# High-part products first, 2048 wide splits and VectorE over both token tiles in the FFN of a diffusion layer

## The chip, the cores and the metric

The kernel runs on one core of one Trainium2 chip. TensorE multiplies, VectorE and ScalarE work element by element, SyncE (SP) issues the transfers, and all five engines run side by side, held together by semaphores. The metric is the device time of one execution in microseconds; the time of a kernel is the median of its runs.

## The reference

One layer of a diffusion backbone on 256 latent tokens of width 2048, in fp32: attention with modulated input, then the SwiGLU feed-forward net (FFN), each with a gated residual and a layer norm. The change touches the FFN:

```python
x = layer_norm(DN_ALPHA * x + g1 * (heads @ w_out[layer]), ln1_g[layer], ln1_b[layer])
u = modulate(x, sh2, sc2)                                   # 256 x 2048
x = layer_norm(DN_ALPHA * x + g2 * ((jax.nn.silu(u @ w_gate) * (u @ w_up)) @ w_down), ln2_g[layer], ln2_b[layer])
```

w_gate and w_up are 2048 x 5632, w_down is 5632 x 2048. sh2, sc2 and g2 are rows of `silu(c) @ w_ada + b_ada`.

## The kernel before, in words

An fp32 product is made of three float32r products: each operand is the sum of a high part (its cast to float32r) and a low part (the rest), and `mm3` adds hi x high, lo x high and hi x low into one accumulator. The activations are the stationary operand of TensorE (`lhsT`, 128 x 128), the weights the moving one (128 x 512). The activations' parts are `u2h` and `u2l` for gate and up, `hTh` and `hTl` for the down projection; `fh` and `fl` hold sums of them (below).

The weights come in tiles of 4 x 128 rows by 512 columns, 1 MB, which SyncE loads into `raw` (four buffers). `split_raw` makes the two parts of a tile in two pieces of 1024: for each, ScalarE casts it into a `hi` tile (L331) and VectorE subtracts that into a `lo` tile (L332). The pool `whl` has four slots each for `hi` and `lo`, 1024 wide. A cast into a slot waits for the last matmul that read the slot's previous content; a load into `raw` waits for the subtraction that read it last. A tile makes 24 matmuls: 4 row blocks x 2 token tiles (`NT`, the 256 tokens are two tiles of 128) x 3.

Until about 400 us a planner (`Flow`) sets the order of attention. Behind it the FFN is written out in the order of the program, and the tile framework's scheduler places the instructions on each engine and puts in the semaphores. Its stages are:

- `first_half`: the first row blocks of gate and up (`project`), beside the steps that make the modulation. The sums go to `spill` tiles.
- Five pairs of 512 wide gate and up columns (`f0` = 0, 2, 4, 6, 8). In each a `folded` generator does four row blocks by four of the gate in 7 instead of 8 products (a Strassen-like scheme); its pieces are 1024 wide, 6 matmuls each, and VectorE makes sums of the weights in `raw` in between. The tiles of `up` run in between (`between`), then the other gate tiles. `shared` adds one of the seven products to the second gate's spill, once per token tile. `residual_base` loads ln1's scale and bias into the single buffer `lgb` (two loads, each spread over all partitions) and makes the base of the residual of 512 columns, with two operations per token tile (L1491, L1492). It is called four times, ahead of the pairs 4, 6 and 8, and the scheduler has drawn all four forward into the first pair.
- `flip_steps`: the gated product of gate and up, a transpose through a scratch buffer in HBM (`put`, `get`), and `place`, which splits the transposed tile into `hTh` and `hTl`, once per token tile.
- The down projection in four groups of 512 output columns (`down_steps`, `last_steps`), with two more `folded` pairs (`down_pair`). `gate2_steps` makes the rows of g2 beside it in four steps of 512: VectorE sums rows of `w_ada` into `adav`, and `split_rows` splits and sums them with a matrix of ones (L478, L479).
- In `last_steps` the last three tiles (`g0` to `g0 + 2`) are multiplied by g2 as weights, and accumulate into banks that ScalarE has filled with the residual (`seed`, L1901). `ending` is the last layer norm.

## Time and profile before

| | |
|---|---|
| device time, median of 3 runs | 1123.49 us (1122.72 to 1123.51) |
| span of the profiled execution | 1121.0 us |
| TensorE busy | 1102.3 us (98%) |
| VectorE busy | 903.4 us (81%) |
| ScalarE busy | 598.7 us (53%) |
| TensorE's share of the chain that ended last | 91% |
| mean share of the 16 DMA engines for the loads' queue | 81.7% |

The span reaches from the first instruction to the last; the device time is that of the whole execution, with what lies around it, so the two are 2.5 us apart. A busy TensorE is not one at its peak, since matmuls overlap; how many start in a stretch says more. Idle time of an engine costs only where another waits for it.

### The profile page before, as it was taken

What the parts mean: (1) busy time and instruction counts of PE and PEld (TensorE: products, weight loads), DVE (VectorE), ACT (ScalarE), POOL (GpSimd) and SP (SyncE); (2) the same over time, 40 slices, a digit from 0 to 9 for tenths busy, and PEclk for the clock granted to TensorE, in tenths of its full rate; (3) what the DMA queues carried; (4) which work ended last, traced back from release to release, by engine and by line L of the source; (5) the groups of instructions that cost most, each with busy time, mean ns of one, the idle gap of its engine ahead of it and who ended that gap; (6) DMA issues with size and microseconds to landing.
All of it is one profiled execution on the core that took longest, in us unless ns stands there. A gap on an engine that the chain in (4) does not pass through costs nothing.

```text
span 1121.0 us, 14130 instructions
## 1 busy us (share of the span) xinstructions
PE 1102.3 (98%) x5213; PEld 883.7 (79%) x5213; DVE 903.4 (81%) x1133; ACT 598.7 (53%) x875; POOL 36.7 (3%) x82
## 2 busy tenths in 40 slices
PE   8999999999999999999999999999999999999995
PEld 6766688777887788888888878888888888888884
DVE  5763589899999888787778697988996987689876
ACT  3341554878685356444475565767766344444442
POOL 1000030110100001000000000000000000000000
PEclk9999999999999999999999999999999999999998
DMA  9999999778999778999956677777776998669742
GB/s 321 394 385 375 393 362 377 247 234 274 345 332 395 249 269 321 348 318 296 336 182 216 223 220 266 234 246 271 228 267 216 329 348 293 228 235 379 287 149 76
DMA packets 178317, 321.26 MB, mean 287 GB/s; under 512 B 8732, under 2 KB 43196, under 8 KB 175943
## 3 DMA queue, kind: packets, MB, share of 16 engines
q1 hardware_dynamic: 177528, 320.03, 81.7%
q8 instruction: 41, 0.67, 0.2%
q10 hardware_dynamic: 720, 0.33, 0.1%
q14 instruction: 28, 0.23, 0.1%
HBM read 304.07 MB, written 16.25 MB: 286 GB/s over the span
## 4 chain that ended last, share of the span: by engine, by line
PE 91%; DMA 3%; DVE 2%; ACT 1%; SPq 1%; issue 0%; ACTq 0%; DVEq 0%
PE acc L341 20%; PE acc L343 20%; PE acc L342 20%; PE wk L342 8%; PE wk L341 8%; PE wk L343 8%; PE wk L1081 2%; PE wk L654 2%; DMA raw<-in_w_in_dram 2%; DVE lo L332 1%; DMA lgb<-in_ln_g_dram 1%; PE wk L755 1%; SPq L569 1%; DMA xt<-in_x_dram 0%; PE wk L1414 0%
## 5 line engine op out<-in xcount | busy, mean ns | idle before, releaser
L331 ACT CAST hi<-raw 128x1024 fp32r<-128x1024 f32 x279 | 290.7, 1054 | 256.4 <-PE acc L343 162.4
L332 DVE TENSOR_TENSOR lo<-raw,hi 128x1024 fp32r<-128x1024 f32 x279 | 336.1, 1220 | 103.6 <-ACT hi L331 101.4
L341 PE MATMUL acc<-hi,u2h 128*128 128x512 f32 x390 | 152.5, 391 | 0.0
L343 PE MATMUL acc<-hi,u2l 128*128 128x512 f32 x390 | 151.7, 390 | 0.7 <-DVE u2l L1669 0.7
L342 PE MATMUL acc<-lo,u2h 128*128 128x512 f32 x390 | 151.8, 389 | 0.0
L603 ACT CAST hi<-raw 128x1024 fp32r<-128x1024 f32 (+1 forms) x86 | 87.4, 1030 | 113.8 <-DMA raw<-in_w_in_dram 63.2
L466 DVE SCALAR_TENSOR_TENSOR adav<-raw,cs,adav 128x512 f32<-128x512 f32 (+1 forms) x128 | 121.4, 949 | 8.4 <-DMA raw<-in_w_ada_dram 4.9
L606 DVE TENSOR_TENSOR lo<-raw,hi 128x1024 fp32r<-128x1024 f32 (+1 forms) x86 | 101.3, 1194 | 16.3 <-ACT hi L603 15.5
L341 PE MATMUL acc<-hi,uh 128*128 128x512 f32 x256 | 103.7, 405 | 1.3 <-ACT uh L769 0.8
L342 PE MATMUL wk<-lo,u2h 128*128 128x512 f32 x264 | 103.1, 390 | 0.5 <-DVE lo L332 0.5
L343 PE MATMUL wk<-hi,u2l 128*128 128x512 f32 x264 | 102.7, 389 | 0.0
L341 PE MATMUL wk<-hi,u2h 128*128 128x512 f32 x264 | 102.2, 389 | 0.0
L342 PE MATMUL acc<-lo,uh 128*128 128x512 f32 x256 | 100.5, 392 | 0.6 <-DVE lo L606 0.6
L343 PE MATMUL acc<-hi,ul 128*128 128x512 f32 x256 | 100.1, 391 | 0.4 <-DVE ul L784 0.4
L341 PE MATMUL acc<-hi,hTh 128*128 128x512 f32 x236 | 92.0, 390 | 0.4 <-ACT acc L1901 0.4
L342 PE MATMUL acc<-lo,hTh 128*128 128x512 f32 x236 | 91.8, 389 | 0.0
L343 PE MATMUL acc<-hi,hTl 128*128 128x512 f32 x236 | 91.8, 389 | 0.0
L343 PEld LDWEIGHTS acc<-hi,u2l 128*128 128x128 f32 x390 | 73.2, 188 | 16.2 <-DVE u2l L1669 1.1
L341 PEld LDWEIGHTS acc<-hi,u2h 128*128 128x128 f32 x390 | 73.2, 188 | 16.1 <-ACT u2h L1668 0.8
L342 PEld LDWEIGHTS acc<-lo,u2h 128*128 128x128 f32 x390 | 73.2, 188 | 15.1
L341 PEld LDWEIGHTS acc<-hi,uh 128*128 128x128 f32 x256 | 48.1, 188 | 19.0 <-issue 5.6
L342 PEld LDWEIGHTS wk<-lo,u2h 128*128 128x128 f32 x264 | 49.5, 188 | 12.0 <-DVE lo L332 1.8
(277 smaller groups left out, 1748.0 us busy)
## 6 DMA issues: line engine op xcount, KB each, us to landing
raw<-in_w_ada_dram SPq DMA_DIRECT2D x70, 1024.0 KB, 7.7
raw<-in_w_gate_dram SPq DMA_DIRECT2D x44, 1024.0 KB, 6.7
raw<-in_w_up_dram SPq DMA_DIRECT2D x44, 1024.0 KB, 5.6
raw<-in_w_down_dram SPq DMA_DIRECT2D x44, 1024.0 KB, 5.8
raw<-in_w_ada_dram SPq DMA_DIRECT2D x48, 512.0 KB, 5.9
raw<-in_w_in_dram SPq DMA_DIRECT2D x18, 1024.0 KB, 11.0
raw<-in_w_out_dram SPq DMA_DIRECT2D x16, 1024.0 KB, 6.5
pd<-hx SPq DMA_DIRECT2D x64, 128.0 KB, 3.4
```

The costliest lines, as they stand in the source:

```text
L331: nc.scalar.copy(hi[:, :n], raw[:, s : s + n])
L332: nc.vector.tensor_tensor(lo[:, :n], raw[:, s : s + n], hi[:, :n].bitcast(F32), op=ALU.subtract)
L341: nc.tensor.matmul(ps, lhsT=xh, rhs=w[0], start=first, stop=False, skip_group_check=seeded)
L342: nc.tensor.matmul(ps, lhsT=xh, rhs=w[1], start=False, stop=False, skip_group_check=seeded)
L343: nc.tensor.matmul(ps, lhsT=xl, rhs=w[0], start=False, stop=last, skip_group_check=seeded)
L466: nc.vector.scalar_tensor_tensor(a[:, c : c + piece], raw[:, f : f + piece], cs[:, 4 * (g * (G4 * NB // w) + j) + 2, None], a[:, c : c + p ...
L569: nc.sync.dma_start(room.t, w[k0 * P : (k0 + 1) * P, c0 : c0 + width])
L603: nc.scalar.copy(hl.hi[:, :n], raw.t[:, s : s + n])
L606: nc.vector.tensor_tensor(hl.lo[:, :n], raw.t[:, s : s + n], hl.hi[:, :n].bitcast(F32), op=ALU.subtract)
L654: nc.tensor.matmul(bank.t[32 * j : 32 * j + 32, :width], lhsT=cs[:, 4 * k + 2 - 2 * i : 4 * k + 34 - 2 * i], rhs=raw.t[:, c * width : (c + ...
L755: nc.tensor.transpose(ps.t[:, (j * 2 + t) * P : (j * 2 + t + 1) * P], src, ident)
L1081: nc.tensor.matmul(o_ps.t[:, : 2 * P].rearrange("p (g q) -> p g q", q=32), lhsT=v, rhs=pv[:, k], start=k == 0, stop=k == 3)
```

## The change

It has three parts. `products` takes the place of `mm3` in the FFN: for a tile it issues all matmuls with the high part of the weights, with both parts of the activations, then those with the low part. `split_raw` casts and subtracts a whole tile of 2048 in one instruction each, into a pair of neighbouring slots of one tile per part, `parts`, with four slots of 1024; `part_pair` hands them out in turn, and a 2048 wide piece starts at an even slot. (Pieces of 1024, as in `folded`, and the rows of 512 take one slot each; the planner gives its casts planned slots.) And `residual_base`, `shared`, the gated product and `place` treat both token tiles in one instruction; `gate2_steps` has two steps of 1024 instead of four of 512.

```diff
-    whl = ctx.enter_context(tc.tile_pool(name="whl", bufs=HL_BUFS))
+    whl = ctx.enter_context(tc.tile_pool(name="whl", bufs=1))
...
+    parts = {c: whl.tile([P, HL_BUFS, SUB * NB], F32R, tag=c, name=c) for c in ("hi", "lo")}
+    turns = [0]
+
+    def part_pair(n):
+        wide = SUB * NB
+        if n > wide:
+            turns[0] += turns[0] % 2
+        i = turns[0] % HL_BUFS
+        turns[0] += -(-n // wide)
+        return [parts[c].rearrange("p b n -> p (b n)")[:, i * wide : i * wide + n] for c in ("hi", "lo")]
...
     def split_raw(raw, spare=False):
-        for s in range(0, raw.shape[-1], SUB * NB):
+        for s in range(0, n, SUB * NB if spare else n):
...
-                hi = whl.tile([P, SUB * NB], F32R, tag="hi", name="hi")
-                lo = whl.tile([P, SUB * NB], F32R, tag="lo", name="lo")
-            nc.scalar.copy(hi[:, :n], raw[:, s : s + n])
-            nc.vector.tensor_tensor(lo[:, :n], raw[:, s : s + n], hi[:, :n].bitcast(F32), op=ALU.subtract)
+                hi, lo = part_pair(n)
+            split(hi, lo, raw[:, s : s + m])
...
+    def products(banks, w, first, last, seeded=False):
+        for j, x in enumerate(banks):
+            for i, (ps, xs) in enumerate(x):
+                for h in xs:
+                    nc.tensor.matmul(ps, lhsT=h, rhs=w[j][0], start=first and not seeded and j == 0 and h is xs[0], stop=False,
+                                     skip_group_check=seeded)
+        for j, x in enumerate(banks):
+            for ps, xs in x:
+                nc.tensor.matmul(ps, lhsT=xs[0], rhs=w[j][1], start=False, stop=last and j == len(banks) - 1,
+                                 skip_group_check=seeded)
...
     def residual_base(n):
...
-        for t in range(NT):
-            nc.vector.scalar_tensor_tensor(xt[:, t, sl], xt[:, t, sl], ALPHA, lg, op0=ALU.mult, op1=ALU.mult)
-            nc.vector.scalar_tensor_tensor(xt[:, t, sl], lb, ALPHA, xt[:, t, sl], op0=ALU.mult, op1=ALU.add)
+        both = xt[:, :, sl]
+        lg, lb = (v[:, None, :].to_broadcast([P, NT, NB]) for v in (lg, lb))
+        nc.vector.scalar_tensor_tensor(both, both, ALPHA, lg, op0=ALU.mult, op1=ALU.mult)
+        nc.vector.scalar_tensor_tensor(both, lb, ALPHA, both, op0=ALU.mult, op1=ALU.add)
...
-        def products(ps, m, piece, first):
-            w = split_raw(piece)
-            for j in range(2):
-                mm3(ps, *forms[m][j], w[j], first and j == 0, j == 1, not first)
+        def product(ps, m, piece, first):
+            products([[(ps, forms[m][j])] for j in range(2)], split_raw(piece), first, True, not first)
...
-    def place(f, t, hf):
+    def place(f, hf):
...
         def shared(e):
-            for t in range(NT):
-                sg = spills[f0 + 1][0][:, t, :]
-                nc.vector.tensor_tensor(sg, sg, e, op=ALU.add)
+            sg = spills[f0 + 1][0]
+            nc.vector.tensor_tensor(sg, sg, e[:, None, :].to_broadcast([P, NT, NB]), op=ALU.add)
...
-    def gate2_steps(n):
-        return ada_rows(5 * D + n * NB, g2sb[:, n * NB : (n + 1) * NB], lambda: vector_sums(NB))
+    def gate2_steps(h):
+        return ada_rows(5 * D + h * 2 * NB, g2sb[:, h * 2 * NB : (h + 1) * 2 * NB], lambda: vector_sums(2 * NB))
...
         def mms(ps, g, t):
-            for j in range(4):
-                k = g * 4 + j
-                mm3(ps, hTh[g][:, j, t * P : (t + 1) * P], hTl[g][:, j, t * P : (t + 1) * P], ws[g][j],
-                    False, k == KF - 1 or k == (ng - TAIL) * 4 - 1, True)
+            products([[(ps, hidden_tokens(g, j, t))] for j in range(4)], ws[g], False, g in (ng - 1, ng - TAIL - 1), True)
```

How the order of the instructions moves, at three places. A row is a line of the kernel, the operation, out<-in by the program's names and the shape; x2 is two such in a row.

First TensorE in `down_steps(0)`, where the rows of gate2 come in (`onesr` is the matrix of ones). Before, high and low parts alternate, and the rows of gate2 (`onesr`) stand between two tiles:

```order
L341 MATMUL acc<-hi,hTh 128x512
L342 MATMUL acc<-lo,hTh 128x512
L343 MATMUL acc<-hi,hTl 128x512
L478 MATMUL wk<-hi,onesr 128x512
L479 MATMUL wk<-lo,onesr 128x512
L341 MATMUL wk<-hi,hTh 128x512
L342 MATMUL wk<-lo,hTh 128x512
L343 MATMUL wk<-hi,hTl 128x512
L341 MATMUL wk<-hi,hTh 128x512
```

In the changed kernel near the same place, the end of one tile and the start of the next; the second row is the tile's last product with a high part:

```order
L364 MATMUL acc<-hi,hTh 128x512
L364 MATMUL acc<-hi,hTl 128x512
L368 MATMUL wk<-lo,hTh 128x512
L368 MATMUL acc<-lo,hTh 128x512
L368 MATMUL wk<-lo,hTh 128x512
L368 MATMUL acc<-lo,hTh 128x512
L368 MATMUL wk<-lo,hTh 128x512
L368 MATMUL acc<-lo,hTh 128x512
L368 MATMUL wk<-lo,hTh 128x512
L368 MATMUL acc<-lo,hTh 128x512
L364 MATMUL wk<-hi,hTh 128x512
```

The eight low-part products now stand together at the tile's end, and the first high-part product of the next tile is the ninth matmul behind the last one of this tile. These two tiles have the same pair of slots, because the rows of gate2 take two slots each time.

Then VectorE in the pairs of columns, at the loads of `lgb`. Before, the last two of the four blocks of `residual_base` stand there:

```order
L1491 SCALAR_TENSOR_TENSOR xt<-xt,lgb 128x512 x2
L1492 SCALAR_TENSOR_TENSOR xt<-lgb,xt 128x512
L332 TENSOR_TENSOR lo<-raw,hi 128x1024
L1492 SCALAR_TENSOR_TENSOR xt<-lgb,xt 128x512
L332 TENSOR_TENSOR lo<-raw,hi 128x1024 x3
L1753 TENSOR_TENSOR spill<-spill,wk 128x512 x2
L332 TENSOR_TENSOR lo<-raw,hi 128x1024 x4
L1491 SCALAR_TENSOR_TENSOR xt<-xt,lgb 128x512 x2
L332 TENSOR_TENSOR lo<-raw,hi 128x1024
L1580 TENSOR_TENSOR spill<-spill,wk 128x512
L1580 TENSOR_TENSOR spill<-spill,acc 128x512
L1492 SCALAR_TENSOR_TENSOR xt<-lgb,xt 128x512
```

In the changed kernel the first two blocks (its operations are L1521 and L1522, 2 x 512 wide):

```order
L356 TENSOR_TENSOR lo<-raw,hi 128x2048
L1521 SCALAR_TENSOR_TENSOR xt<-xt,lgb 128x2x512
L356 TENSOR_TENSOR lo<-raw,hi 128x2048
L1522 SCALAR_TENSOR_TENSOR xt<-lgb,xt 128x2x512
L356 TENSOR_TENSOR lo<-raw,hi 128x1024 x2
L1588 TENSOR_TENSOR raw<-raw 128x1024
L1595 TENSOR_TENSOR raw<-raw 128x1024
L1521 SCALAR_TENSOR_TENSOR xt<-xt,lgb 128x2x512
L356 TENSOR_TENSOR lo<-raw,hi 128x2048
L356 TENSOR_TENSOR lo<-raw,hi 128x1024
L1792 TENSOR_TENSOR spill<-spill,wk 128x1024
L1522 SCALAR_TENSOR_TENSOR xt<-lgb,xt 128x2x512
```

Between the second operation of a block, which is the last to read `lgb`, and the first of the next block, which needs it loaded anew, stood nine instructions before, of 512 and 1024; now there are four. The fourth block stood among the last instructions of the first pair of columns (L1580 is its `gated_half`); now it ends five instructions ahead of that.

And ScalarE in the tail, from the last tiles of the down projection on. Before:

```order
L331 CAST hi<-raw 128x1024 x15
L331 CAST hilo<-raw 128x1024
L331 CAST hi<-raw 128x1024
L331 CAST hilo<-raw 128x1024
L331 CAST hi<-raw 128x1024
L1901 COPY acc<-xt 128x512
L331 CAST hi<-raw 128x1024
L1901 COPY acc<-xt 128x512
```

In the changed kernel:

```order
L355 CAST hi<-raw 128x2048
L510 COPY room<-wk 128x512
L355 CAST hi<-raw 128x2048 x7
L355 CAST hilo<-raw 128x1024 x2
L355 CAST hi<-raw 128x2048
L1926 COPY acc<-xt 128x512 x2
```

The cast of `hilo` is that of the last tile, which goes into spare buffers. Ahead of the first copy that fills an accumulator (`acc<-xt`) stood a cast of 1024, and a second one between the two copies; now one cast of 2048 stands ahead of both.

## Rows read from the trace of the kernel before

**Rows 1.** The page's part 1: busy time, share of the span, instructions.
```profile
PE 1102.3 (98%) x5213; PEld 883.7 (79%) x5213; DVE 903.4 (81%) x1133; ACT 598.7 (53%) x875; POOL 36.7 (3%) x82
```

**Rows 2.** Stages: PE, PEld, DVE, ACT, POOL busy us (x); PEclk, DMA share, GB/s.
```profile
404.00:1090.00 686.00, 685.46 (x3049) 565.22 (x3048) 561.16 (x595) 370.88 (x444) 6.59 (x14) 1.00 0.79 270
448.00:476.00 28.00, 28.00 (x125) 23.18 (x124) 21.62 (x19) 13.76 (x16) 0.00 (x0) 1.00 0.99 345
645.76:669.34 23.58, 23.04 (x99) 18.16 (x98) 22.67 (x25) 13.64 (x18) 0.00 (x0) 1.00 0.71 220
593.70:598.00 4.30, 4.30 (x21) 3.56 (x20) 3.20 (x5) 2.11 (x2) 0.00 (x0) 1.00 0.54 123
784.00:812.00 28.00, 28.00 (x126) 23.17 (x125) 27.87 (x32) 20.12 (x27) 0.00 (x0) 1.00 0.71 221
```

**Rows 3.** Timeline of TensorE (start us, us, engine, line, operation, tiles) in the first half.
```profile
480.66 0.39 PE L341 MATMUL acc<-hi,u2h 128*128 128x512 f32 x1
480.88 0.39 PE L342 MATMUL acc<-lo,u2h 128*128 128x512 f32 x1
481.11 0.39 PE L343 MATMUL acc<-hi,u2l 128*128 128x512 f32 x1
481.34 0.39 PE L341 MATMUL acc<-hi,u2h 128*128 128x512 f32 x1
```

**Rows 4.** Timeline of TensorE at one of three waits between 645 and 670 us.
```profile
653.04 0.39 PE L341 MATMUL wk<-hi,u2h 128*128 128x512 f32 x1
653.80 0.50 PE L342 MATMUL wk<-lo,u2h 128*128 128x512 f32 x1 [0.37 <-DVE lo L332]
654.14 0.40 PE L343 MATMUL wk<-hi,u2l 128*128 128x512 f32 x1
```

**Rows 5.** Chain of waits, 560 to 700 us (start us, us, what).
```profile
627.12 9.63 DMA lgb<-in_ln_g_dram
```

**Rows 6.** Timeline of VectorE behind that load.
```profile
636.78 1.29 DVE L1491 SCALAR_TENSOR_TENSOR xt<-xt,lgb 128x512 f32<-128x512 f32 x2 [4.77 <-DMA lgb<-in_ln_g_dram]
```

**Rows 7.** Timeline of TensorE in the fold of the down projection.
```profile
1001.12 0.40 PE L342 MATMUL acc<-lo,hTh 128*128 128x512 f32 x1
...
1001.69 0.39 PE L343 MATMUL wk<-hi,hTl 128*128 128x512 f32 x1
```

**Rows 8.** Costliest weight loads (PEld): group xcount | busy us, mean ns | idle before.
```profile
L342 PEld LDWEIGHTS acc<-lo,u2h 128*128 128x128 f32 x390 | 73.2, 188 | 15.1
```

**Rows 9.** VectorE's groups by shape from 404 us, the same columns.
```profile
L332 DVE TENSOR_TENSOR lo<-raw,hi 128x1024 fp32r<-128x1024 f32 x278 | 334.9, 1220 | 103.6 <-ACT hi L331 101.4
L1891 DVE TENSOR_TENSOR raw<-raw,room 128x2048 f32<-128x2048 f32 x3 | 6.9, 2287 | 0.1
```

**Rows 10.** ScalarE's groups by shape from 404 us, the same columns.
```profile
L331 ACT CAST hi<-raw 128x1024 fp32r<-128x1024 f32 x277 | 288.7, 1054 | 255.2 <-PE acc L343 161.1 <-PE wk L343 43.1 <-DMA raw<-in_w_down_dram 16.5
L337 ACT CAST hTh<-spill 128x512 fp32r<-128x512 f32 x20 | 12.0, 620 | 5.2 <-DMA spill<-hd 5.0
```

**Rows 11.** Timeline of TensorE and ScalarE near 999 us: a slot is released.
```profile
999.02 0.39 PE L343 MATMUL acc<-hi,hTl 128*128 128x512 f32 x1
...
999.45 1.05 ACT L331 CAST hi<-raw 128x1024 fp32r<-128x1024 f32 x1 [0.23 <-PE acc L343]
```

**Rows 12.** Timeline of TensorE and ScalarE in the tail.
```profile
1091.98 1.05 ACT L331 CAST hi<-raw 128x1024 fp32r<-128x1024 f32 x1
...
1092.78 0.39 PE L343 MATMUL acc<-hi,hTl 128*128 128x512 f32 x1
1092.93 0.58 ACT L1901 COPY acc<-xt 128x512 f32<-128x512 f32 x1
...
1093.56 0.50 PE L341 MATMUL acc<-hi,hTh 128*128 128x512 f32 x1 [0.40 <-ACT acc L1901]
...
1093.90 0.40 PE L342 MATMUL acc<-lo,hTh 128*128 128x512 f32 x1
```

More of the change, by code (lines that the diff above doesn't have):

```diff
@@ L259, in run @@
     def run(self):
-        for s, s.start, pools in self.search()[0]:
+        best = self.search()[0]
+        free = [(0.0, i) for i in range(self.room["hl"])]
+        left = {b: b.left for s, _, _ in best for b in s.give}
+        for s, s.start, pools in best:
             for b, b.pool in zip(s.take, pools):
-                pass
+                if b.pool == "hl":
+                    free.sort()
+                    b.slot = free.pop(0)[1]
+            for b in s.give:
+                left[b] -= 1
+                if left[b] == 0 and b.pool == "hl":
+                    free.append((s.start + s.ns, b.slot))
             s.fn()
@@ L600, in cast @@
                 else:
-                    hl.hi = whl.tile([P, SUB * NB], F32R, tag="hi", name="hi")
-                    hl.lo = whl.tile([P, SUB * NB], F32R, tag="lo", name="lo")
+                    hl.hi, hl.lo = (parts[c][:, hl.slot, :] for c in ("hi", "lo"))
                 nc.scalar.copy(hl.hi[:, :n], raw.t[:, s : s + n])
@@ L1489, in residual_base, with tokens @@
         nc.sync.dma_start(lb, ln1_b[0:1, sl].to_broadcast([P, NB]))
-        for t in range(NT):
-            nc.vector.scalar_tensor_tensor(xt[:, t, sl], xt[:, t, sl], ALPHA, lg, op0=ALU.mult, op1=ALU.mult)
-            nc.vector.scalar_tensor_tensor(xt[:, t, sl], lb, ALPHA, xt[:, t, sl], op0=ALU.mult, op1=ALU.add)
-    def project(accs, w_, f, g, first, last, seeded=False):
-        w = load_split(w_, g * 4, f * NB)
-        for j in range(4):
-            k = g * 4 + j
-            for t in range(NT):
-                mm3(accs[t], u2h[:, k, t * P : (t + 1) * P], u2l[:, k, t * P : (t + 1) * P], w[j],
-                    k == first and not seeded, k == last, seeded)
+        both = xt[:, :, sl]
+        lg, lb = (v[:, None, :].to_broadcast([P, NT, NB]) for v in (lg, lb))
+        nc.vector.scalar_tensor_tensor(both, both, ALPHA, lg, op0=ALU.mult, op1=ALU.mult)
+        nc.vector.scalar_tensor_tensor(both, lb, ALPHA, both, op0=ALU.mult, op1=ALU.add)
+    def tokens(k, t):
+        return tuple(u[:, k, t * P : (t + 1) * P] for u in (u2h, u2l))
+    def project(accs, w_, f, g, first, last, seeded=False):
+        w = split_raw(load_raw(w_, g * 4, G4, f * NB, NB))
+        products([[(accs[t], tokens(g * 4 + j, t)) for t in range(NT)] for j in range(4)], w, g * 4 == first, g * 4 + 3 == last, seeded)
     def sums(a11, a21, a12, a22):
@@ L1553, in folded @@
         tt = nc.vector.tensor_tensor
-        products(a, 11, b11, True)
+        product(a, 11, b11, True)
         b = acc_bank()
@@ L1558, in folded @@
         yield
-        products(e, 1, b11, True)
+        product(e, 1, b11, True)
         tt(b12, b22, b12, op=ALU.subtract)
@@ L1562, in folded @@
         yield
-        products(b, 2, b11, False)
+        product(b, 2, b11, False)
         c = acc_bank()
@@ L1566, in folded @@
         shared(e)
-        products(a, 12, b21, False)
+        product(a, 12, b21, False)
         tt(b21, b21, b11, op=ALU.subtract)
         yield
-        products(c, 3, b12, False)
+        product(c, 3, b12, False)
         d = acc_bank()
         nc.scalar.copy(d, c)
-        products(b, 4, b22, False)
+        product(b, 4, b22, False)
         yield
-        products(c, 22, b21, False)
+        product(c, 22, b21, False)
         yield (a, c), (b, d)
@@ L1606, in place, with flip_steps @@
             hTl[f] = pb.tile([P, 4, SEQ], F32R, tag=f"hTl{f}", name="hTl")
-        hi, lo = (h[f][:, :, t * P : (t + 1) * P].rearrange("p q (a i) -> p q a i", a=4) for h in (hTh, hTl))
-        split(hi, lo, hf.rearrange("p (a q i) -> p q a i", a=4, q=Q))
-    def flip_steps(f, up, hh, hx, late):
+        hi, lo = (h[f].rearrange("p q (b i) -> p q b i", i=32) for h in (hTh, hTl))
+        split(hi, lo, hf.rearrange("p t (a q i) -> p q (t a) i", a=4, q=Q))
+    def flip_steps(f, up, hh, hx, late, wide):
         def gated(t):
-            nc.vector.tensor_mul(hh[t], up[t], hh[t])
+            if not late:
+                nc.vector.tensor_mul(hh[t], up[t], hh[t])
+            elif t == 0:
+                nc.vector.tensor_mul(wide, spills[f][1], wide)
             squares(hh[t], hx[t])
@@ L1630, in places @@
         def places():
-            for t in range(NT):
-                place(f, t, hf[t])
+            place(f, wide)
             if f == FOLD_H:
@@ L1850, in share, with hidden_tokens @@
             nc.vector.tensor_add(xt[:, t, sl], xt[:, t, sl], hx[0])
+    def hidden_tokens(g, j, t):
+        return tuple(h[g][:, j, t * P : (t + 1) * P] for h in (hTh, hTl))
     def down_step(n, g):
[L1854 to L1858 removed]
+        w = split_raw(load_raw(w_down, g * 4, G4, n * NB, NB))
+        products([[(accs[n][t], hidden_tokens(g, j, t)) for t in range(NT)] for j in range(4)], w, False, g * 4 + 4 == KF, True)
         turn()
@@ L1935, in dit_layer @@
     accs[2], accs[3] = next(it)
[L1936 removed]
+    run(merge(down_steps(2), gate2_steps(1)))
     run(merge(last_steps(), [lambda: share(3, extra2[0]), l2_loads]))
```

31 lines of the change are left out of this document (10 added, 21 removed).

## The prediction

> **What bounds the kernel now.** I read the page's shares first: TensorE is busy 1102.3 of 1121.0 us, VectorE 81%, ScalarE 53% [rows 1]. Whatever shortens VectorE or ScalarE alone can give back only what TensorE waits. So the next view is the table by stage. From 404 to 1090 us, the FFN, which is nearly all that the change touches, TensorE is busy 685.46 of 686.00 us at a granted clock of 1.00 [rows 2], the upper of its two levels, 2.4 GHz. A stretch without a wait holds 125 matmuls in 28 us [rows 2], and the timeline shows one every 0.227 us, each 0.39 us long because they overlap [rows 3]. The step is the same when the stationary tile stays (L341 to L342, both with u2h: 0.22 and 0.23) as when it changes (L342 to L343, L343 to L341: 0.23) [rows 3]. The change leaves the number of matmuls alone; some 3,070 of them get a new order.
>
> What TensorE loses now in this stage: from 645.76 to 669.34 us the table counts 99 matmuls, of which one had begun before [rows 2]; 98 steps of 0.2267 are 22.2, so 1.36 us are waits, at three places. One is shown [rows 4]: the matmul that is due at 653.27 starts at 653.80, and the next follows after 0.34 instead of 0.23; a wait costs its length plus 0.11. It waits for a subtraction (`lo`), and the chain of waits says why that is late: 9.63 us for the load of ln1's scale into `lgb` [rows 5], which held VectorE idle for 4.77 us at 636.78 [rows 6] with all later subtractions behind it. Three more waits lie near 930, 999.7 and 1001.4, of 0.14, 0.04 and 0.12 us (the last: 0.57 for two steps instead of 0.45 [rows 7]). Then one at 1093.56, near the end (below). Little can be won: some 2.4 us in all.
>
> **Part 1, the order in `products`.** All high-part products of a tile (16) now run before its low-part products (8). At the measured step that is worth nothing by itself. What it moves is slack: a subtraction may now end 16 steps (3.6 us) after its cast's first use, where before it had to be there one step later. VectorE's lateness as in [rows 4] is covered by that. But the last high-part product of a tile is now its 16th of 24, and the cast that reuses the slot may start there.
>
> A rule speaks against this order. The Trainium skill ("TensorE: Matmul & The Clock Gate", "What happens when you issue a matmul") says that a stationary operand can be loaded once and used by many matmuls; before, two of three products in a row had the same one, now neighbours never have. By that rule a third of the products would gain a load. The trace shows as many weight loads as matmuls already (390 for L342 alone, the second of the pair), 188 ns each [rows 8], shorter than the 227 ns step that covers them: price 0. If the cover were gone, a third of 3,070 loads at 188 ns would be 192 us; I give that 0.02.
>
> **Part 2, one cast and one subtraction of 2048.** VectorE: 1.22 us for 1024, 2.29 for a 2048 wide operation [rows 9], so a pair saves some 0.15 us of duration, and its covers are TensorE's full windows [rows 2]: worth 0. ScalarE has no 2048 row. From 0.62 us at 512 and 1.05 at 1024 [rows 10], the slope is 0.85 ns per element, so 1.05 + 1024 x 0.00085 = 1.92 us at 2048; the upper bound is two casts of 1024, 2.11, the lower the slope alone, 1.74. I take 1.92, since the two rows lie on its line. (The Trainium skill, "ScalarE: Activation LUTs", "What ACT_TABLE_LOAD costs", has 186 ns plus 0.833 ns per element, an estimate of 1.89 us; each of the waits below would be 0.03 shorter.)
>
> TensorE now waits until all 2048 columns are done, where it waited for 1024. The shortest chain from the last use of a slot to the first use of the new tile: matmul 0.39, release 0.04 (the product at 999.02 ends at 999.41, the cast starts at 999.45 [rows 11]), cast 1.92, start of the matmul 0.05 (copy ends 1093.51, matmul starts 1093.56 [rows 12]); sum 2.40 us, or 10.6 steps. Wherever the new program has fewer steps between the two, TensorE stands. I counted them in the two programs' orders:
> - Once 7 steps, at the first 2048 tile (about 404 us, behind the planned part, whose order is the same in both kernels): 2.40 - 1.59 = 0.81, plus 0.11: **+0.92**.
> - Three times 9 steps (2.04 us): where the rows of gate2 take two slots and two neighbouring tiles get the same pair (about 930 and 1048 us), and once in the fold near 999: 3 x (0.36 + 0.11) = 1.41, less the 0.30 lost at 930 to 1002 now: **+1.1**. Bounds with the cast at 1.74 and 2.11: 0.6 and 1.7; the first place 0.74 and 1.11.
> - Twenty times 15 steps (3.40 us): 1.0 us in hand when ScalarE is free. Value 0, bound below.
> - All others 17 or more (mostly 33). Before, the smallest was 15 steps, for a cast of 1.05.
>
> **Part 3, both token tiles in one instruction.** `residual_base`, `shared`, the gated product and `place` save VectorE some 30 instructions; covered as above, 0. But the four `lgb` loads move. Now they are spread to 627 us, the last behind three weight loads; in the new order all four blocks stand within the first pair of columns, each with four VectorE instructions or fewer behind the release of the single buffer. The late load at 627 goes, and with it the waits at 645 to 669: **-1.3** (bounds 0 and -1.36). Queued behind each new wait are the subtractions of that stretch. For how long: a pair of these loads holds the queue for 4.3 us at 123 GB/s [rows 2]; with one weight load ahead the scale lands some 4 to 5 us after issue. The tightest is the second pair: four instructions of about 1.2 us hide it, and by my count along TensorE's steps the 2048 wide subtraction behind it then ends 1.7 us before the low part needs it. Value 0.
>
> **Part 4, the tail.** In `last_steps` ScalarE now does 1024 wide casts around the copy that seeds the first of the last two accumulators: cast at 1091.98, copy at 1092.93, matmul at 1093.56 instead of 1093.01 (0.55 + 0.11) [rows 12]. The new order has one 2048 cast ahead of that copy, and it is released by the product at 1091.87 (four steps before 1092.78): 1091.87 + 0.39 + 0.04 = 1092.30, end 1094.22; the copy follows 0.10 before the end as now, at 1094.12, takes 0.58, and the matmul starts at 1094.75 instead of 1093.01: 1.74 + 0.11. Difference **+1.2** (with 2.11 for the cast +1.4, with 1.74 +1.0). Behind this there is nothing to absorb it: TensorE runs to the end. gate2 in two steps of 1024 instead of four: VectorE only, 0.
>
> **Sum.** 0.92 + 1.1 - 1.3 + 1.2 = +1.9 us on a span of 1121.0. The median of the runs is 2.49 above this span: 1125.4 us.
>
> **The rivals.**
> 1. *The folds stall* (slower). In them the 2048 tiles have only one slot pair, and 784 to 812 us show VectorE busy 27.87 of 28 [rows 2]. For it: the 1.0 us in hand at 15 steps is less than one 2048 cast ahead of it in ScalarE's queue. Against it: before, with the same load, TensorE lost nothing from 700 to 900. It decides when a cast starts over 1.0 us late; one whole cast late is 1.92 - 1.0 + 0.11 = 1.0. One to three such places: 1126.4 to 1128.4.
> 2. *The `lgb` loads hold VectorE in the first pair* (slower). It decides when the second pair's load takes over 4.3 + 1.7 = 6 us from issue to landing. At the 9.63 of [rows 5] that subtraction would come 3.6 us too late, and with it the fourth pair's about as much: up to 7 in all, 1127 to 1132. Against it: that load had three weight loads ahead of it, these have one.
> 3. *The step of a matmul falls* (faster). High-part neighbours share the moving tile; should that shorten the step by 1.5 ns, 3,070 steps give back 4.6 us, 1120.8. From 1.4 ns on it is faster by over 0.2%. Against it: L343 and the L341 of the next triple, and L341 and L342, differ in what they share, and the steps do not [rows 3].
> 4. *The short chains don't bite*, because the scheduler's distances leave more than I count or the cast is quicker: only tail and `lgb` remain, 1123.4.
>
> **How the numbers follow.** A change of under 0.2% (2.25 us) can't be told from none here; the limits are 1121.2 and 1125.7. My sum 0.52, with its own range 1124.4 to 1126.4 from the bounds of the cast (to 1127.7 if the waits at 645 stay; 0.37 of its chance below 1125.7); rival 1 0.20, rival 2 0.12, rival 3 0.07, rival 4 0.07, weight loads 0.02. Faster 0.07, same 0.37 + 0.07 = 0.44, slower 0.15 + 0.20 + 0.12 + 0.02 = 0.49. The range 1123.0 to 1129.0 leaves out rival 3, the weight loads and some two thirds of rival 2: 0.17.
>
> **What the changed profile would show.** Right: matmul step 0.227 in hi and lo stretches alike; a wait of 0.8 us near 404 and three of 0.4 for the 2048 cast, with ScalarE as releaser; none from 645 to 669; one of 1.7 before the first product into that accumulator, released by the copy. Wrong: waits for `lo` in the first fold with a load of `lgb` behind them (rival 2), waits for the cast or the subtraction between 680 and 900 (rival 1), a step other than 0.227 (rival 3), or a cast far from 1.92.

## The result and the profile after

The changed kernel takes 1125.84 us (median of 22 runs, 1123.70 to 1127.36) against 1123.22 for the kernel before (22 runs, 1120.63 to 1126.13): ratio 1.0025, 95% interval 1.0019 to 1.0031, so 2.1 to 3.5 us slower. The profiled execution of the changed kernel has a span of 1123.9 us, that of before 1121.0.

The page's first part, which answers to [rows 1], and the stage from 404 to 1090 us, which answers to the first row of [rows 2]:

```profile
PE 1102.4 (98%) x5213; PEld 883.1 (79%) x5213; DVE 882.8 (79%) x952; ACT 577.7 (51%) x749; POOL 43.9 (4%) x80
```

```profile
404.00:1090.00 686.00, 684.75 (x3047) 564.89 (x3046) 539.98 (x414) 351.09 (x320) 14.62 (x12) 1.00 0.78 270
```

VectorE is 20.6 us less busy and ScalarE 21.0, and TensorE's busy time is the same: what the two engines were relieved of gave TensorE nothing. The step of a matmul did not move either, neither among the products with the high part (neighbours share the moving tile) nor among those with the low part: in TensorE's timeline 7 steps from 479.95 to 481.54 and 8 from there to 483.35 are 0.226 to 0.227 us each, as in [rows 3].

```profile
479.95 0.39 PE L364 MATMUL acc<-hi,u2l 128*128 128x512 f32 x1
480.18 0.39 PE L364 MATMUL acc<-hi,u2h 128*128 128x512 f32 x1
480.40 0.39 PE L364 MATMUL acc<-hi,u2l 128*128 128x512 f32 x1
...
481.54 1.98 PE L368 MATMUL acc<-lo,u2h 128*128 128x512 f32 x8
483.35 0.39 PE L364 MATMUL acc<-hi,u2h 128*128 128x512 f32 x1
```

The difference lies in TensorE's waits. The view of waits, TensorE alone, 380 to 1120 us (line that waited, what it waited for; us in total, times, longest):

```profile
PE acc L364 <- ACT acc L1926: 1.6, 1, 1.6
PE acc L374 <- DVE u2l L1698: 0.7, 1, 0.7
PE acc L364 <- ACT hi L355: 0.6, 1, 0.6
PE wk L364 <- ACT hi L355: 0.6, 3, 0.2
```

The second of these is in both kernels. The others are new or larger, and each stands behind a 2048 wide cast, the second group here (VectorE's subtraction is the first):

```profile
L356 DVE TENSOR_TENSOR lo<-raw,hi 128x2048 fp32r<-128x2048 f32 x115 | 262.7, 2288 | 109.8 <-ACT hi L355 109.6
L355 ACT CAST hi<-raw 128x2048 fp32r<-128x2048 f32 x115 | 220.2, 1915 | 278.1 <-PE acc L364 151.2 <-PE wk L364 52.8 <-DMA raw<-in_w_down_dram 28.1
```

The first 2048 wide tile in the timeline: the cast starts when a slot is released and holds the next product, which was due at 404.87, one step behind 404.64, and starts 0.80 late. (The 0.64 in brackets counts from the end of the matmul before, 0.39 behind its start; the text counts from the due start.) The product behind it comes after 0.34 instead of 0.227, which is another 0.11; a wait is given below as 0.80 + 0.11.

```profile
403.70 1.91 ACT L355 CAST hi<-raw 128x2048 fp32r<-128x2048 f32 x1 [0.28 <-PE acc L374]
...
404.64 0.39 PE L374 MATMUL acc<-hi,u2l 128*128 128x512 f32 x1
...
405.67 0.50 PE L364 MATMUL acc<-hi,u2h 128*128 128x512 f32 x1 [0.64 <-ACT hi L355]
...
406.00 0.39 PE L364 MATMUL acc<-hi,u2l 128*128 128x512 f32 x1
```

Of the three waits in the last row of the view of waits, the second is the longest, 0.40 + 0.11; the other two are 0.35 + 0.11, at 929.65 and 1049.94:

```profile
999.88 0.39 PE L368 MATMUL acc<-lo,hTh 128*128 128x512 f32 x1
1000.50 0.50 PE L364 MATMUL wk<-hi,hTh 128*128 128x512 f32 x1 [0.23 <-ACT hi L355]
1000.84 0.40 PE L364 MATMUL wk<-hi,hTl 128*128 128x512 f32 x1
```

And the tail, which answers to [rows 12]: one 2048 cast stands ahead of the copy that fills the accumulator. The product was due at 1094.67, five steps behind the first row, and starts 1.74 late.

```profile
1093.54 0.39 PE L364 MATMUL acc<-hi,hTl 128*128 128x512 f32 x1
...
1093.96 1.91 ACT L355 CAST hi<-raw 128x2048 fp32r<-128x2048 f32 x1
1094.41 0.69 DVE L1925 TENSOR_TENSOR xt<-xt,room 128x512 f32<-128x512 f32 x1
...
1095.78 0.58 ACT L1926 COPY acc<-xt 128x512 f32<-128x512 f32 x1
...
1096.40 0.50 PE L364 MATMUL acc<-hi,hTh 128*128 128x512 f32 x1 [1.57 <-ACT acc L1926]
```

### The profile page after: what moved, and what is told of

Read it like the earlier page. It is cut to its first block, busy times and chain, and to the rows that moved or that the text cites. A ratio compares the mean times of both kernels' runs of the same rounds, so it can differ in the third digit from the quotient of the medians.

```text
span 1123.9 us, 13751 instructions
## 1 busy us (share of the span) xinstructions
PE 1102.4 (98%) x5213; PEld 883.1 (79%) x5213; DVE 882.8 (79%) x952; ACT 577.7 (51%) x749; POOL 43.9 (4%) x80
## 4 chain that ended last, share of the span: by engine, by line
PE 91%; DMA 5%; ACT 2%; DVE 2%; issue 0%; SPq 0%; ACTq 0%; DVEq 0%
PE acc L364 27%; PE wk L364 15%; PE acc L368 13%; PE wk L368 7%; PE acc L372 7%; PE acc L374 7%; PE acc L373 7%; DMA raw<-in_w_in_dram 3%; PE wk L1110 2%; PE wk L683 2%; DMA raw<-in_w_ada_dram 2%; ACT hi L355 1%; PE wk L372 1%; PE wk L374 1%; PE wk L373 1%; DVE g1b L497 1%
## 5 line engine op out<-in xcount | busy, mean ns | idle before, releaser
L355 ACT CAST hi<-raw 128x2048 fp32r<-128x2048 f32 (+1 forms) x164 | 271.3, 1659 | 303.3 <-PE acc L364 165.3
L356 DVE TENSOR_TENSOR lo<-raw,hi 128x2048 fp32r<-128x2048 f32 (+1 forms) x164 | 320.5, 1968 | 117.9 <-ACT hi L355 110.3
L364 PE MATMUL acc<-hi,u2h 128*128 128x512 f32 x374 | 145.7, 391 | 0.6 <-ACT hi L355 0.6
L364 PE MATMUL acc<-hi,u2l 128*128 128x512 f32 x374 | 145.3, 389 | 0.0
L497 DVE SCALAR_TENSOR_TENSOR adav<-raw,cs,adav 128x1024 f32<-128x1024 f32 (+1 forms) x96 | 114.4, 1192 | 10.2 <-DMA raw<-in_w_ada_dram 7.6
L368 PE MATMUL acc<-lo,u2h 128*128 128x512 f32 x374 | 97.0, 389 | 0.0
L364 PEld LDWEIGHTS acc<-hi,u2h 128*128 128x128 f32 x374 | 70.2, 188 | 15.6 <-ACT hi L355 1.1
L368 PE MATMUL acc<-lo,hTh 128*128 128x512 f32 x236 | 71.4, 389 | 0.0
L368 PE MATMUL wk<-lo,u2h 128*128 128x512 f32 x264 | 70.4, 389 | 0.0
L364 PEld LDWEIGHTS wk<-hi,u2l 128*128 128x128 f32 x264 | 49.6, 188 | 10.3
```

Source lines behind the costliest of these rows:

```text
L355: nc.scalar.copy(hi, src)
L356: nc.vector.tensor_tensor(lo, src, hi.bitcast(F32), op=ALU.subtract)
L364: nc.tensor.matmul(ps, lhsT=h, rhs=w[j][0], start=first and not seeded and j == 0 and h is xs[0], stop=False, skip_group_check=seeded)
L368: nc.tensor.matmul(ps, lhsT=xs[0], rhs=w[j][1], start=False, stop=last and j == len(banks) - 1, skip_group_check=seeded)
L497: nc.vector.scalar_tensor_tensor(a[:, c : c + piece], raw[:, f : f + piece], cs[:, 4 * (g * (G4 * NB // w) + j) + 2, None], a[:, c : c + p ...
```

## The experiments

A profile is one execution, and executions of one kernel do not start alike: the wait on `u2l` (second row of the waits above), which every kernel here has and behind which the part with the change begins, comes at 398.59 in the first profile of before and between 398.65 and 399.88 in three others. So I compare two things: the times, and in the traces the stretch from the end of that wait to the end of the last instruction. For three of four profiles of before this stretch is 720.81 to 720.85 us; the last column is the difference to 720.83.

| kernel | median, before beside it (us) | ratio, 95% interval | that is, us | stretch (us) | over 720.83 |
|---|---|---|---|---|---|
| before, profile shown above | 1123.22 | | | 722.44 | +1.6 |
| before_again, before_2, before_3 | 1123.53, 1123.01 (first of them) | 1.0002, 0.9992 to 1.0011 | -0.9 to +1.2 | 720.82, 720.81, 720.85 | 0 |
| changed | 1125.84, 1123.22 | 1.0025, 1.0019 to 1.0031 | +2.1 to +3.5 | 724.21 | +3.4 |
| after_2 (changed, again) | 1130.12, one run | | | 724.19 | +3.4 |
| seed_direct | 1124.47, 1122.52 | 1.0015, 1.0006 to 1.0024 | +0.7 to +2.7 | 722.97 | +2.1 |
| half_four_direct | 1123.16, 1122.52 | 1.0002, 0.9993 to 1.0011 | -0.8 to +1.2 | 721.38 | +0.6 |
| hi_first_1024 | 1123.89, 1122.52 | 1.0012, 1.0002 to 1.0021 | +0.2 to +2.4 | 722.30 | +1.5 |
| slots_only | 1122.94, 1123.01 | 1.0007, 0.9998 to 1.0016 | -0.2 to +1.8 | 721.58 | +0.7 |
| before_merged_base | 1122.80, 1123.01 | 1.0000, 0.9991 to 1.0009 | -1.0 to +1.0 | 721.19 | +0.4 |
| slow_lgb | 1129.37, 1123.01 | 1.0059, 1.0044 to 1.0074 | +4.9 to +8.3 | 727.86 | +7.0 |
| before_slow_lgb | 1123.99, 1122.53 | 1.0014, 1.0003 to 1.0026 | +0.3 to +2.9 | 721.67 | +0.8 |
| wide_triples | 1269.04, one run | | | 864.96 | +144 |

With this zero, every difference in the stretch lies inside the interval of the times. It was not the zero that I had: the forecast was made against the first profile, 722.44.

**The tail without the copy: seed_direct.** In the changed kernel VectorE writes the residual straight into the accumulator.

```diff
-            nc.vector.tensor_add(xt[:, t, sl], xt[:, t, sl], yts[t])
-            nc.scalar.copy(whole[t], xt[:, t, sl])
+            nc.vector.tensor_add(whole[t], xt[:, t, sl], yts[t])
```

> The changed kernel, but in the tail VectorE's addition writes the residual straight into the accumulator, and ScalarE's copy (behind the 2048 wide cast) is gone. Chain theory: the wait of 1.74 us before the first product into that accumulator was the copy queued behind the cast; now the matmul waits for the addition alone, which ended at 1095.10 in the changed kernel's trace, so it starts at 1095.15 instead of 1096.40 (due 1094.66): a wait of 0.5 us, and the kernel is 1.25 us faster than the changed one (about 1124.6 us). Rival: the wait there only moves (to the low part's subtraction or to the end), then the same time as the changed kernel, 1125.8.

The wait fell from 1.74 + 0.11 to 0.59 + 0.08, and the stretch by 1.24. The 2048 cast still stands there, but nothing waits for it now:

```profile
1092.62 1.91 ACT L355 CAST hi<-raw 128x2048 fp32r<-128x2048 f32 x1
1093.08 0.69 DVE L1925 TENSOR_TENSOR acc<-xt,room 128x512 f32<-128x512 f32 x1
...
1093.91 0.47 PE L364 MATMUL acc<-hi,hTh 128*128 128x512 f32 x1 [0.42 <-DVE acc L1925]
```

So the copy, with its place behind a cast that does not concern it, makes 1.15 of the 1.74. Not all of this is the place. The copy needs the sum that VectorE's addition writes (L1925 in the tail above), and that ended at 1095.10, 0.43 behind the due time of the product; the copy lost 0.68 us behind the cast, to 1095.78, and takes 0.58 itself. In the kernel before, the addition ended 0.7 us ahead of the due time (1093.01):

```profile
1091.62 0.69 DVE L1900 TENSOR_TENSOR xt<-xt,room 128x512 f32<-128x512 f32 x1
```

In the changed kernel a subtraction of `hilo` of 1.22 us stands between VectorE's multiplication and this addition, and before it did not. That puts the addition later, and seed_direct's remaining 0.59 is the wait for it. With the cast out of the way and the copy kept, some 1.1 us of wait would be left (an estimate: 0.43 + 0.58 + 0.05); no run tried that order.

**Four tiles halved: half_four_direct.** On top of that, the tiles behind the four short chains (no. 1, 86, 97 and 106) are split in two pieces of 1024; the other 2048 wide ones stay.

```diff
+HALVES = (1, 86, 97, 106)
...
+        if n > SUB * NB and not spare:
+            turns[0] += turns[0] % 2
+            tiles[0] += 1
+            half = tiles[0] in HALVES
+        step = SUB * NB if spare or half else n
```

> As seed_direct, and the four tiles whose slots are released 7 or 9 steps ahead of their first use are cast and subtracted in two pieces of 1024, all others in one of 2048. Chain theory: a cast of 1024 makes the chain 0.39 + 0.04 + 1.06 + 0.05 = 1.54 us, under 7 steps (1.59), so the four waits (0.91, 0.46, 0.51, 0.46 with what follows each) go: 2.3 us more than seed_direct, about 1122.3 us, 0.9 us below the kernel before. Rival: the excess over the kernel before is spread (a longer start, many tiles of 15 steps), then it stays at 1124.6 or ends above the kernel before.

The three waits near 930, 1000 and 1050 are gone; the first tile keeps 0.50 + 0.11 of its 0.80 + 0.11. The stretch falls by another 1.59: 1.43 at the three places, 0.30 at the first tile and 0.05 of a small one near 1057, less two new ones of 0.11 and 0.09 near 436 and 998. In time the kernel is no longer to be told from before; the 0.9 us below it that I expected did not come. I had the first tile's wait of 0.91 go too, of which 0.30 went, and I counted from the medians, by which the changed kernel is 2.6 us over before, where the stretch has 3.4. What is left at the first tile stands behind two casts of 1024 back to back: the product starts at the end of the second (405.25), so halving the tile doesn't bring it to one cast of 1024.

```profile
403.24 2.01 ACT L364 CAST hi<-raw 128x1024 fp32r<-128x1024 f32 x2
...
405.30 0.50 PE L373 MATMUL acc<-hi,u2h 128*128 128x512 f32 x1 [0.34 <-ACT hi L364]
```

**High part first, but all pieces 1024 wide: hi_first_1024.**

```diff
-        for s in range(0, n, SUB * NB if spare else n):
-            m = SUB * NB if spare else n
+        if n > SUB * NB and not spare:
+            turns[0] += turns[0] % 2
+        step = SUB * NB if spare or True else n
+        for s in range(0, n, step):
+            m = step
...
-                hi, lo = part_pair(n)
+                hi, lo = part_pair(m)
```

> The changed kernel with every cast and subtraction 1024 wide again; order of the products and both token tiles in one instruction stay. Chain theory: width is the only part that costs: the four waits go (2.3 us), and in the tail the copy stands behind two casts of 1024 of which the second is released as before, so its matmul is about 0.9 us late instead of 1.74: 0.8 us. Together 3.1 us under the changed kernel, about 1122.7 us. VectorE does 115 instructions more and TensorE hides it. Rival: the merged casts are what VectorE and ScalarE need in the folds; then waits for lo or hi appear between 680 and 900 us and it is no faster than the changed kernel.

Stretch +1.5, time +0.2 to +2.4: 1.9 us below the changed kernel in the stretch where I expected 3.1, so width is not the only part that costs. The rival fails too: TensorE has no wait between 680 and 900 us. The three nine-step waits are gone, but one of 0.22 + 0.11 stands at 931.18; the first tile keeps 0.50 + 0.11 and the tail 0.92 + 0.11 (0.55 + 0.11 before), behind the same copy. Of these the first tile's comes with the new storage (slots_only, below); whether the others come with the order of the products, the slots or the merged instructions is not told apart here.

```profile
1092.69 0.58 ACT L1929 COPY acc<-xt 128x512 f32<-128x512 f32 x1
...
1093.32 0.50 PE L367 MATMUL acc<-hi,hTh 128*128 128x512 f32 x1 [0.76 <-ACT acc L1929]
```

**2048 wide, but the old order: wide_triples.** The body of `products` is a call of `mm3` per row block and bank.

```diff
-                for h in xs:
...
+                mm3(ps, *xs, w[j], first and not seeded and j == 0, last and j == len(banks) - 1, seeded)
```

> The changed kernel with the products in triples again (hi, lo, hi for each row block), the casts still 2048 wide. Chain theory: the low part is then wanted one step after the high part, and a slot is free only after its tile's last product, so release to first use of lo needs 0.39 + 0.04 + 1.92 + 0.03 + 2.29 + 0.05 = 4.7 us, 21 steps, and 33 tiles have 3 to 13 steps: each waits 1.5 to 4 us, 40 to 90 us in all, 1165 to 1215 us; waits named after the subtraction. Rival: the order is worth nothing (TensorE's step is the same and VectorE keeps ahead): within 2 us of the changed kernel.

The direction was right, the size far too small: +144 us in the stretch. TensorE now waits for cast and subtraction one behind the other, longer for the cast (47 us in these rows), where I had named the subtraction (33). These are rows of the waits view from 380 us on:

```profile
PE wk L366 <- ACT hi L355: 31.9, 28, 1.8
PE wk L367 <- DVE lo L356: 27.0, 21, 2.6
PE acc L366 <- ACT hi L355: 15.3, 22, 1.7
PE acc L367 <- DVE lo L356: 6.2, 5, 2.4
```

All its waits there sum to 86 us. By TensorE's start times the other 58 have two parts. Some 30 lie at the edges of the 82 waits, above all the 0.16 from the due start to the end of the matmul before, which the view leaves out, and the 0.11 behind each wait. Some 28 are 142 matmuls behind waits that are slow. Three stretches of it (length, TensorE's busy us, matmuls, granted clock, share of DMA, GB/s):

```profile
786.77:790.12 3.35, 1.39 (x4) 1.00 0.02 7
791.34:793.90 2.56, 2.56 (x7) 0.50 0.88 290
795.04:797.80 2.76, 2.76 (x14) 1.00 0.81 315
```

TensorE starts three matmuls in these 3.35 us (the fourth of the row began before), then runs at a granted clock of 0.50, the lower level of 1.2 GHz, where a matmul starts every 0.43 us, and some 3 us later every 0.23 us again. My expectation had only the waits in it, and those at 40 to 90 us. The run shows what the new order is for: with it the low part has 16 steps; without it the 2048 wide split costs 13% (one run).

**The kernel before, again: before_again, before_2, before_3.** Nothing is edited.

> The kernel before, unchanged, as a measure of what its own executions differ by. All theories: 0 within the interval. Its profile gives a second start: in the first profile the matmul that is number 2045 started at 395.92 us, in four kernels with the change at 397.06, 395.80, 397.00 and 396.12, though the order up to there is the same. If the start is scatter, this one may lie anywhere from 395.5 to 397.3; if the change moves it, it lies at 395.9 or below.

> The kernel before, unchanged, profiled a third time. The forecast took 1.3 us of gain from three waits of TensorE at 645 to 669 us that one profile shows; the second profile of the same kernel shows none there, and its waits from 395 us on sum to 2.8 us instead of 4.3. If those waits are an accident of one execution, this profile shows few or none of them (sum 2.7 to 3.6); if they belong to the kernel and the second profile was the exception, about 1.4 us of waits for lo between 640 and 670.

> The same kernel a fourth time, with the same two expectations; three of four without the waits would make the accident the better reading.

None of the three has a wait between 645 and 669 us, where the first profile has three, and in the stage of the first row of [rows 2] TensorE is busy without a gap; this is before_2, and the other two have the same row:

```profile
404.00:1090.00 686.00, 686.00 (x3056) 1.00 0.79 270
```

VectorE does wait for `lgb` in them, but less: 2.3, 3.6 and 3.3 us in all, where the first profile has 4.77 in one wait [rows 6] and 5.6 in all. The rows of before_3:

```profile
DVE xt L1491 <- DMA lgb<-in_ln_g_dram: 2.4, 1, 2.4
DVE xt L1492 <- DMA lgb<-in_ln_b_dram: 0.9, 1, 0.9
```

The late load is there in all three all the same. It is issued at 627 to 628.5, behind the weights, and the operation of VectorE that needs it starts 6.6, 7.3 and 7.3 us later, as in before_2:

```profile
628.00 0.46 SPq L1488 DMA_DIRECT2D lgb<-in_ln_g_dram  x1
```

```profile
635.25 1.29 DVE L1491 SCALAR_TENSOR_TENSOR xt<-xt,lgb 128x512 f32<-128x512 f32 x2 [2.35 <-DMA lgb<-in_ln_g_dram]
```

So the load's place is the kernel's, and TensorE loses nothing by it at these lengths; the 9.63 us [rows 5] are one execution's, and with them the three waits. The wait of 0.14 near 930 is gone too, and of those at 999.7 and 1001.4 one of 0.07 to 0.11 stays.

**The new storage alone: slots_only.** The kernel before with the tile `parts`, the planner's planned slots and `part_pair`, but the old order and pieces of 1024.

```diff
-                hi = whl.tile([P, SUB * NB], F32R, tag="hi", name="hi")
-                lo = whl.tile([P, SUB * NB], F32R, tag="lo", name="lo")
+                hi, lo = part_pair(n)
```

> The kernel before with only the storage of the change: one tile with four slots per part and the planner's slots, pieces of 1024 in turn, products in triples, each token tile by itself. The three kernels run so far lie 0.9 to 1.7 us above what their waits in the FFN add up to. Start theory: that rest comes from the first 395 us, where only storage and slots are new; then this kernel is 1 to 1.5 us slower than the kernel before, and its matmul 2045 starts near 397. Rival: the rest is scatter, or sits in the FFN where the waits don't show it; then it is 0 within 0.5 us.

I had looked for an extra cost of the storage in the first 395 us, since times lay above what the FFN's waits added up to against the first profile. The time alone doesn't decide (-0.2 to +1.8). Its start is late, with the wait on `u2l` at 400.43, but in before_merged_base, which has the old storage, it is at 401.51, so that is scatter. The trace decides for one place: the first tile waits 0.50 + 0.11, as in hi_first_1024 and half_four_direct, though the program's order and width are those of before:

```profile
406.04 0.97 PE L362 MATMUL acc<-hi,u2h 128*128 128x512 f32 x3 [0.34 <-ACT hi L352]
```

The x3 shows that the scheduler's order is not quite that of before: three products with the high part stand in a row where hi, lo and hi alternated; in all, ten of TensorE's products are drawn forward there from some 7 us behind. So of the 0.91 at the first tile 0.61 comes with the new storage and 0.30 with the width. Whether the slots hold the cast or the order that the scheduler makes of them is not told apart. A cost of storage ahead of that is not needed: with the zero of the table the stretch alone gives the times.

**Merged residual base in the old kernel: before_merged_base.**

```diff
-        for t in range(NT):
-            nc.vector.scalar_tensor_tensor(xt[:, t, sl], xt[:, t, sl], ALPHA, lg, op0=ALU.mult, op1=ALU.mult)
-            nc.vector.scalar_tensor_tensor(xt[:, t, sl], lb, ALPHA, xt[:, t, sl], op0=ALU.mult, op1=ALU.add)
+        both = xt[:, :, sl]
+        lg, lb = (v[:, None, :].to_broadcast([P, NT, NB]) for v in (lg, lb))
+        nc.vector.scalar_tensor_tensor(both, both, ALPHA, lg, op0=ALU.mult, op1=ALU.mult)
+        nc.vector.scalar_tensor_tensor(both, lb, ALPHA, both, op0=ALU.mult, op1=ALU.add)
```

> The kernel before, with only residual_base over both token tiles in one instruction. Load theory: the three waits of 1.3 us between 645 and 670 us came from the fourth load of ln1's rows, issued at 627 behind three weight loads; with two operations a block instead of four the loads come earlier, so the waits go: 1.3 us faster than before. Rival: they went because the high parts run first and the subtractions got slack; then they are still there and the time is that of the kernel before.

Ratio 1.0000: no gain. The waits at 645 to 669 are missing, but so they are without the edit; one of 0.35 + 0.11 came up at 752.85.

**`lgb` loaded twice: slow_lgb and before_slow_lgb.** In both kernels the two loads are issued a second time.

```diff
         nc.sync.dma_start(lg, ln1_g[0:1, sl].to_broadcast([P, NB]))
         nc.sync.dma_start(lb, ln1_b[0:1, sl].to_broadcast([P, NB]))
+        nc.sync.dma_start(lg, ln1_g[0:1, sl].to_broadcast([P, NB]))
+        nc.sync.dma_start(lb, ln1_b[0:1, sl].to_broadcast([P, NB]))
```

> The changed kernel with both loads into lgb issued twice in a row, the same rows again, so that a block of residual_base waits for 8 us or more from issue to landing instead of 4.0 to 4.9. Threshold theory: 6 us are covered; beyond that VectorE stands with the subtractions of the first pair of columns behind it: TensorE waits for lo there, 5 to 6 us behind the second load and 1 to 4 behind the others, 6 to 13 us in all, 1132 to 1139 us. Rival: the 16 steps of slack of the low part cover it, at most 1 us.

The changed kernel loses 3.6 us more in the stretch, where the theory had 6 to 13 and the rival at most 1, and not by the theory. The waits of TensorE from 590 to 630 us are for a cast, not for a subtraction:

```profile
PE wk L364 <- ACT hi L355: 2.3, 2, 1.9
PE wk L364 <- DVE spill L1784: 0.5, 1, 0.5
```

The chain of waits of the same kernel says why the cast is late: the weights' load was issued late, since SyncE stood at the second load of `lgb` until the first had landed, and the weights' load comes behind it.

```profile
607.51 4.73 DMA lgb<-in_ln_b_dram
612.26 0.72 SPq L1520
613.04 7.97 DMA raw<-in_w_up_dram
621.12 1.91 ACT hi L355
```

The edit added a wait on SyncE that it was not meant to add, so it tells what a late weight load costs, and leaves open from how long a load of `lgb` on a late subtraction would hold TensorE (6 us by rival 2).

> The kernel before, in which the two loads of lgb are issued twice each, as in the same edit to the changed kernel, which cost that one 3.5 us. Theory: in the old order a subtraction that comes late behind a late lgb holds TensorE at the very next product, so that the three waits at 645 to 669 come back in every execution, for 1.3 us or more after the last block and perhaps others behind the earlier blocks: 1124 to 1127 us. Rival: the 9.63 us load of the first profile was not what made those waits, and nothing of over 0.3 us is seen there: 1123.

In the old kernel VectorE waits 10.3 us for `lgb` in all, 4.56 of it at once at 623.18, and TensorE waits for `lo` once, right behind that:

```profile
625.06 0.50 PE L342 MATMUL acc<-lo,u2h 128*128 128x512 f32 x1 [0.41 <-DVE lo L332]
```

It costs 0.57 + 0.11; the three waits at 645 to 669 did not come back. In the old order, then, a late `lgb` does reach TensorE, at a size of 0.7 to 1.4 us where VectorE stands for over 4 us at once, and not at all at 2.3 to 3.6 us in two waits (the three executions above).

**The changed kernel again: after_2.**

> The changed kernel, profiled a second time. If its waits are set by the order and the 2048 wide cast alone, every one of them comes back at its place and size: 0.80 near 405, 0.35 to 0.40 at three places, 1.74 in the tail, sum 6.2 us from 395 us on within 0.3. If they hang on how loads land, sizes differ by more than 0.1 us. The start, up to the matmul no. 2045, may differ by up to 3 us either way, as it does between executions of the kernel before.

Every wait from 404 us on came back at the same size to 0.01 us, and the stretch to 0.03. What its time, one run of 1130.12, has over the others lies in the start: the wait on `u2l` comes at 404.15, 4.4 us later than in the first profile. The stage from 0 to 100 us, first the first profile, then this one:

```profile
0.00:100.00 100.00, 94.70 (x635) 1.00 1.01 362
```

```profile
0.00:100.00 100.00, 92.14 (x615) 0.98 0.98 343
```

Fewer bytes came in (343 GB/s for 362) and TensorE issued 20 matmuls less. Why one execution loads more slowly was not tried.

## Why the prediction came out as it did

The forecast, 1125.4 within 1123.0 to 1129.0, and slower by over 0.2% as the likeliest of three, held: 1125.84, ratio 1.0025. By its steps:

- **The order, price 0: right.** Step 0.227 in both parts, 188 ns for a weight load as in [rows 8]. The Trainium skill ("TensorE: Matmul & The Clock Gate", "What happens when you issue a matmul") says that a stationary operand can be loaded once and used by many matmuls, and the prediction kept a charge for the extra loads, drawn from that, as a rival with a chance of 0.02. The same section of the Trainium skill has the next tile's weights load while the current matmul runs, and with this the trace agrees: the loads stay under the step that covers them, and no charge shows. This is the row of the changed kernel:

```profile
L364 PEld LDWEIGHTS acc<-hi,u2h 128*128 128x128 f32 x374 | 70.2, 188 | 15.6 <-ACT hi L355 1.1
```

- **The cast of 2048 at 1.92 us: right**, 1.915. (By the figures of the Trainium skill, "ScalarE: Activation LUTs", "What ACT_TABLE_LOAD costs", 186 ns plus 0.833 ns per element, an estimate would be 1.89; the trace lies 0.02 above.)
- **The first tile, +0.92: right in size** (0.80 + 0.11), wrong in its attribution: I put it down to the width, and 0.61 of it comes with the new storage (slots_only).
- **Three nine-step places: right.** 0.35, 0.40 and 0.35, each with 0.11, near 930, 1000 and 1050: 1.43 against 1.41. half_four_direct splits these tiles, and the waits go.
- **The tail, +1.2: right in size.** 1.74 + 0.11 as worked out, for 0.55 + 0.11 before, and the copy does go last behind the cast. But the working had the queue alone in it. VectorE's addition is late too, by 0.43, and the cast hides that; with the cast's place alone mended, some 1.1 of wait would stay (the estimate under seed_direct). With the copy taken away it is 0.59.
- **`lgb`, -1.3: this step failed.** "The late load at 627 goes, and with it the waits at 645 to 669". The changed kernel has no such waits, but three of four executions of the old one have none either. The gain was read from one execution: the late load is in all four, and cost TensorE something only where it took 9.63 us, not at 6.6 to 7.3. The 0.30 that I subtracted for the small waits from 930 to 1002 is of the same kind; about 0.1 of it recurs. Without both the sum is 0.92 + 1.41 + 1.2 less 0.1, +3.4 instead of +1.9; the stretch shows +3.4, the times +2.1 to +3.5. The bounds of that term (0 to -1.36) had it, the value was at the wrong end.
- **The rivals.** No wait in the folds (rival 1): from 680 to 900 us TensorE lost nothing. No wait for `lo` (rival 2): three of the four loads of the scale land 4.0 to 4.9 us after issue, as estimated; the second pair's, the tightest, was there before VectorE wanted it, 4.7 us after issue. VectorE waits 4.2 us in three waits that nothing passes on. The threshold of 6 us itself stays untested. The step did not fall (rival 3), and the short chains bite (rival 4).

That the time came out 0.4 us from the forecast is partly luck. The sum was 1.5 us short of the +3.4 of the stretch; but the two medians lie only 2.6 us apart, within the interval, and the forecast started from the median of three runs, 1123.49, which is 0.27 above that of 22.

Nothing tried here is faster than the kernel before. half_four_direct, with the changed order and width but without the tail's copy and the three nine-step waits, is level with it.

## What to carry to other kernels

Count, for every tile slot, the engine's steps between the last use of its old content and the first use of the new, and compare with release, cast and start; the few places where they are short set what a wider instruction costs, and they can be split by hand while the rest stays wide. Before a wait seen in one profile is booked as a gain, profile the unchanged kernel again: a wait set by instruction order returned to 0.01 us, one set by a load's landing was there once in four times. An instruction that follows in a queue on a widened one, like the copy in the tail, pays for the width too, even where it has nothing to do with it; but look also at when its own input was ready, since the queue can hide a second lateness.

## What the runs showed of the hardware

- After waits in which TensorE started three matmuls in 3.35 us, its granted clock fell to 0.50, and a matmul started every 0.43 us instead of 0.23 for some 3 us. In wide_triples this came again and again: 142 matmuls were slow by 28 us in all. With some 30 us at the edges of the waits, that made waits of 86 us into a loss of 144.
- Executions of one program differ by up to 4.4 us (changed kernel) in the first 400 us, while the 720 us behind them repeat to 0.04 us (three of four executions of before, both of the changed kernel); the fourth of before, with the load of 9.63 us, is 1.6 us longer.
- A load into `lgb` that took 6.6 to 7.3 us from issue to use, and held VectorE for up to 2.4 us at once, cost TensorE nothing in three executions of the old kernel; where VectorE stood for 4.6 to 4.8 us at once, TensorE lost 0.7 to 1.4.
